# The lower parts of the weights after the attention: a subtraction on VectorE becomes a negation on ScalarE and an adding DMA

## The chip, the cores and the metric

The kernel runs on one core of one Trainium2 chip. The metric is the device time in microseconds of one execution; two runs of the kernel before took 971.85 and 971.94 us (median 971.89). The profile shows one execution of the same program: its engines are PE (TensorE, with PEld for its weight loads), DVE (VectorE), ACT (ScalarE), POOL (GpSimd) and the DMA queues that SP, ACT and POOL issue to (SPq, ACTq, and POOL's own).

## The reference, cut to what matters

One layer of a decoder trunk with three parallel token mixers, all float32, for 512 tokens of 1024 channels:

```
h   = adaLN(RMSNorm(x); c)
P   = h @ W_in                      # 13,872 columns, shared out among the mixers and three merge gates
yA  = gated short convolution       (from P)
yB  = sparse attention, 16 heads    (from P)
yC  = chunked spatial gating        (from P)
m   = sum_i sigmoid(h @ W_g[i]) * (y_i @ W_br[i])      # i = A, B, C
out = x + gate(c) * RMSNorm(m @ W_out)
```

What counts here are the large products. Each is made from operands that are split into two float32r parts: an upper part (the value rounded to float32r) and a lower part (the value less its upper part). A product is then three float32r matmuls: upper by upper, upper by lower, lower by upper.

## The kernel before, in words

The work is a stream of units. A unit is one product with 256 columns of weights: two PSUM banks of 24 matmuls of 128x128 by 512 each, 48 matmuls in all (`chan`, lines 99 to 107; the units with the tokens on the partitions use `tok`, lines 109 to 118, with matmuls of 256 columns). While a unit's matmuls run, the next unit's weights are fetched and split. They come in four pieces of 128x2x256 float32 (256 KB): SP issues a load into one of three `raw` buffers (`load_w`, line 84); then `split` (line 70) makes the upper part `wh` on ACT (line 71) and the lower part `wl` on DVE (line 72), out of `raw` and `wh`. `wh` and `wl` of a unit have two buffers, so that a piece can be split only when the unit before the running one has read its weights to the end. In a unit with `chan`, piece q is first used by the matmuls of blocks k = 2q and 2q+1, and `wl` by the third matmul of each block (line 106).

`split` also serves other operands: attention weights, keys, and the mixers' outputs (`yh`, `yl`). PE's order is that in which the code is written; the order on ACT, DVE, POOL and the queues is made by a scheduler with its own timing model.

The program goes: start (norm, adaLN, first products), the attention with projections of `h` filled in between its steps, and, from line 726 on, a second half: eight units for branch A (four gates `u_gate`, four merges `u_merge`), four units `u_v2`, eight units `u_z2` and `u_u2`, eight units for branch B, eight for branch C, then the output projection with the weights `woh` and `wo2` (lines 925 to 958). Between branch A's units the second half also loads `ws`, which POOL masks (`affine_select`, line 857), and `bi` and `gpb`. During branch B, `gate` (line 884) loads 16 more pieces of 256 KB into `rawg`; during branch C, `load_wo` (line 909) loads eight pieces of `w_out`.

Names of lines that the prediction uses: 71 and 72 (the two instructions of `split`), 84 (loads of pieces), 102, 104, 106 (the three matmuls of `chan`), 747 (drain of a gate's bank on ACT), 857 (mask of `ws` on POOL).

Of the kernel before, what the change touches and what calls it, by code (L numbers as in the profile page):

```python
# [10 lines left out]
AF = mybir.ActivationFunctionType  # L11
OP = mybir.AluOpType
# [25 lines left out]
def hybrid_block(ctx, tc, x, c, g_pre, g_post, w_ada, b_ada, w_in, conv_w, conv_b, pos_ck, w_ck1, w_ck2,  # L38
                 pos_cv, w_cv1, w_cv2, ln_g, ln_b, w_s, b_s, w_br, w_out, out):
    nc = tc.nc  # L40
    act = nc.scalar.activation
    stt = nc.vector.scalar_tensor_tensor
    ts = nc.vector.tensor_scalar
    tt = nc.vector.tensor_tensor
# [5 lines left out]
    w_ada = w_ada[0]  # L50
# [17 lines left out]
    WP, RB = 2, 3  # L68
# [1 line left out]
    def split(dst_h, dst_l, src):  # L70
        act(dst_h, src, AF.Copy)  # L71
        tt(dst_l, src, dst_h, op=OP.subtract)  # L72

# [4 lines left out]
    def load_w(src, col):  # L78
        """Starts the load of 256 columns; what comes back with the tiles are the steps that split them."""
        w = w_tiles()  # L80
        steps = []
        for q in range(0, KT, WP):
            raw = wpool.tile([128, WP, 256], F, name="raw", bufs=RB)
            nc.sync.dma_start(raw, src[q * 128:(q + WP) * 128, col:col + 256].rearrange("(k p) c -> p k c", p=128))
            steps.append((w[0][:, q:q + WP, :], w[1][:, q:q + WP, :], raw))
        return w, steps

    def rsqrt(y, v, neg_half):
        """y = v ** -0.5 by Newton's steps from a bitwise first guess; all [128, n]."""
        ts(y.bitcast(I32), v.bitcast(I32), -0.5, 1597463007.0, op0=OP.mult, op1=OP.add)  # L90
        ts(neg_half, v, -0.5, None, op0=OP.mult)
        t = const.tile(list(y.shape), F, name="rsq_t", bufs=2)
        for _ in range(3):
            tt(t, y, y, op=OP.mult)
            tt(t, t, neg_half, op=OP.mult)
            stt(y, t, 1.5, y, op0=OP.add, op1=OP.mult)

# [1 line left out]
    def chan(ps, w, sub, rh, rl, ks=range(KT), m=128):  # L99
# [19 lines left out]

    # ================= pools of the first half =================  # L120
    att = ExitStack()
# [5 lines left out]

    # ================= start: rmsnorm, adaLN, h transposed =================
    crow = sp.tile([KT, 128], F, name="crow")
# [41 lines left out]
    def load_ada(n, part):  # L171
        """Columns of w_ada for scale and shift of the channels of group n."""
        k, cnt = groups[n]
        per = 4 // cnt
        wa = sp.tile([128, per, 2, cnt * 128], F, name="wa", bufs=6)
        for e, off in enumerate((D, 0)):
            nc.sync.dma_start(wa[:, :, e, :], w_ada[part * per * 128:(part + 1) * per * 128,
                                                    off + k * 128:off + (k + cnt) * 128].rearrange(
                "(k p) c -> p k c", p=128))
        for q in range(per):  # L180
            was[n, part * per + q] = wa[:, q]
# [16 lines left out]
    def root(i):  # L198
        """The steps of ssq's way to its inverse root."""
        if i == 0:  # L200
            ts(ssq, ssq, 1.0 / D, EPS, op0=OP.mult, op1=OP.add)
        elif i == 1:
            ts(rst.bitcast(I32), ssq.bitcast(I32), -0.5, 1597463007.0, op0=OP.mult, op1=OP.add)
            ts(nh, ssq, -0.5, None, op0=OP.mult)
        elif i % 3 == 2:
            tt(ssq, rst, rst, op=OP.mult)
        elif i % 3 == 0:
            tt(ssq, ssq, nh, op=OP.mult)
        else:
            stt(rst, ssq, 1.5, rst, op0=OP.add, op1=OP.mult)  # L210
# [24 lines left out]
    def ada(n, q):  # L235
        """A step of the sum over c's channels for group n."""
        if n not in accs:
            accs[n] = sp.tile([128, 2, groups[n][1] * 128], F, name="acc", bufs=2)
            ts(accs[n], was[n, q], csil[:, q:q + 1], None, op0=OP.mult)
        else:  # L240
            stt(accs[n], was[n, q], csil[:, q:q + 1], accs[n], op0=OP.mult, op1=OP.add)
# [28 lines left out]
    def product(k, j, p):  # L270
        """One of the three passes of block k's share of two blocks of channels."""
        for e in range(2):
            mm(first[j][e], w_first[j][p == 1][:, k, e * 128:e * 128 + 128], (hh, hh, hl)[p][:, k, :],  # L273
               start=(todo[j] == 3 * KT), stop=(todo[j] == 1))
        todo[j] -= 1
# [21 lines left out]

    # ================= constants and long-lived tiles of the attention =================
    D0 = const.tile([128, S], F, name="D0")
# [56 lines left out]

# [1 line left out]
    class Stream:  # L358
# [20 lines left out]
        def step(self, last=False):  # L379
            """One matmul further; False at the end (or at that of the unit, if it is the last)."""  # L380
            while True:
# [26 lines left out]
        def to(self, n):  # L408
            """Through the first n units."""
            while self.n < n or (self.n == n and self.gen is not None):  # L410
                if not self.step(self.n == n):
                    break
# [10 lines left out]
    def w_vg():  # L423
        """The window's values and the gates' logits, side by side."""
        w = (gv.tile([128, KT, 304], R, name="wvh"), gv.tile([128, KT, 304], R, name="wvl"))
        steps = []
# [30 lines left out]

    # ================= compressed keys and values, among the projections =================
    def cmp_hidden(b):
# [45 lines left out]

    # ================= attention =================
    keep = ctx.enter_context(tc.tile_pool(name="keep", bufs=1, side="right", reuse_waits="tile"))
# [10 lines left out]

    # gated convolution branch (as twice its value)
    def u_cg(w, j):  # L520
# [22 lines left out]
    def u_silu(w, j, ys):  # L543
        """ys times twice the silu of the projection."""
        for e in range(2):
            b = 2 * j + e
            ps = acc_tile()
            yield from chan(ps, w, e, hh, hl)
            th = wk.tile([128, S], F, name="th", bufs=2)
            act(th, ps, AF.Tanh, scale=0.5)  # L550
            stt(th, th, 1.0, ps, op0=OP.add, op1=OP.mult)
            tt(ys[b], ys[b], th, op=OP.mult)
# [13 lines left out]

    # the keys of a group: for each branch 32 places for the compressed ones (the selected branch has them)
    # and then its own, upper parts and lower parts
    def k_stack(g, b):
# [34 lines left out]

    # the compressed branch's weights, transposed: a partition for each key, four times: upper and lower
    # parts of the even and of the odd blocks of queries; the rest of a row stays zero
    pcs = [wk.tile([128, NB // 2, 2, 128], R, name=f"pc{n}") for n in range(2)]
# [16 lines left out]
    def scores(u, i):  # L624
        """The scores of the queries' block i; for the first block those of both branches at once."""
        h, b = divmod(u, 2)
# [3 lines left out]
        ks = kst[h // HPG]  # L630
        # a bank has no room for the last block's compressed scores: they are with the first's
        o = 32 if b == 0 and i < NB - 1 else 0
# [54 lines left out]

    # the projections that run among the attention's steps, and the one that can only follow them
    base = len(stream.units)
# [8 lines left out]

    # positions of a unit's steps (head and branch), in periods from the unit's first
    POS = dict(S0=-1.301, S1=-0.333, S2=-0.131, S3=0.070, T0=0.701, T1=0.875, V0=1.510, V1=1.562, T2=1.261, T3=1.137, V2=1.802, V3=1.872, CS=0.718, CT=0.622, CO=1.177, HO=1.920, QS=-2.289, K0=-3.502, K1=-3.559)  # L700
# [22 lines left out]
    stream.to(len(stream.units))  # L723
    att.close()

    # ================= merge of the branches =================
    po = ctx.enter_context(tc.tile_pool(name="po", bufs=1, reuse_waits="tile"))
# [45 lines left out]

    # ================= gated spatial branch (as twice its value) =================
    def gelu_tanh(ps):
# [100 lines left out]

    # ================= the other branches; gate of the layer, times g_post =================
    fin = ctx.enter_context(tc.tile_pool(name="fin", bufs=1, reuse_waits="tile"))
# [44 lines left out]

    # ================= output projection, rmsnorm, residual =================
    wo2 = []
# [8 lines left out]
    for t in range(NB):  # L934
# [4 lines left out]
        bank = [acc_tile() for _ in parts]  # L939
        # as the parts come: their squares' sums, and their products with the gates  # L940
        for n, (cs, ps, wh, wl) in enumerate(zip(
# [47 lines left out]
```

## Time and profile before

| | |
|---|---|
| runs | 971.85 and 971.94 us |
| span of the profiled execution | 969.5 us; the runs' median is 2.4 us above it |
| PE busy | 939.7 us (97%) |
| DVE busy | 640.3 us (66%) |
| ACT busy | 447.7 us (46%) |
| POOL busy | 13.4 us (1%) |
| granted TensorE clock, mean | 0.999 |

The span is the time from the first to the last instruction of the profiled execution; the runs' time also holds what lies around it. Busy shares are means over the whole program, so the stages have to be read apart. The DMA engines' busy share is that of the core's 16 engines together. A wait is put down to the instruction that ended it.

### The profile page before, as it was taken

How to read it: one execution, taken by the hardware profiler on the slowest of the kernel's cores; microseconds unless marked ns; L12 is line 12 of the kernel's file. 1: busy time of each engine (PE TensorE's matmuls, PEld its weight loads, DVE VectorE, ACT ScalarE, POOL GpSimd, SP SyncE). 2: the span in 40 equal slices, each digit the busy share in tenths (PEclk: the TensorE clock that was granted, in tenths of full speed). 3: DMA queues.
4: the chain of work that ended last, by engine and by line, in shares of the span. 5: the costliest groups of instructions: out<-in, count | busy, mean ns of one | idle time of the engine just before them, and what ended most of it. 6: DMA issues, size and time to landing. Idle time of an engine off the chain costs nothing.

```text
span 969.5 us, 13657 instructions
## 1 busy us (share of the span) xinstructions
PE 939.7 (97%) x4833; PEld 797.1 (82%) x4833; DVE 640.3 (66%) x1641; ACT 447.7 (46%) x982; POOL 13.4 (1%) x38
## 2 busy tenths in 40 slices
PE   2999999999999999999999999999999999999996
PEld 1788978888887888888888888998888888888896
DVE  5863387998998889989855325666554654844443
ACT  5552366676666656666534224333333323523311
POOL 2010000000000000000000000000000000000000
PEclk9999999999999999999999999999999999999999
DMA  9963112222131221213134333233335545432312
GB/s 288 310 173 102 44 44 71 61 56 76 44 88 44 58 74 47 85 44 88 44 88 152 92 114 92 84 90 95 87 88 157 180 141 152 151 90 87 98 59 94
DMA packets 98569, 97.76 MB, mean 101 GB/s; under 512 B 6808, under 2 KB 93956, under 8 KB 98500
## 3 DMA queue, kind: packets, MB, share of 16 engines
q1 hardware_dynamic: 96132, 92.51, 32.8%
q10 hardware_dynamic: 2048, 4.19, 1.3%
q8 instruction: 38, 0.62, 0.3%
q14 instruction: 31, 0.25, 0.1%
q0 software_dynamic: 320, 0.17, 0.1%
HBM read 94.76 MB, written 2.10 MB: 100 GB/s over the span
## 4 chain that ended last, share of the span: by engine, by line
PE 92%; DMA 4%; DVE 2%; ACT 1%; SPq 1%; issue 0%; DVEq 0%; ACTq 0%
PE g L102 21%; PE g L104 21%; PE g L106 21%; PE o L678 4%; PE t L667 4%; PE s L645 3%; PE g L113 2%; PE g L117 2%; PE g L115 2%; DMA wa<-in_w_ada_dram 2%; PE s L463 2%; PE g L947 2%; PE g L948 2%; PE g L946 2%; PE f L273 2%; PE t L821 1%
## 5 line engine op out<-in xcount | busy, mean ns | idle before, releaser
L102 PE MATMUL g<-hh,wh 128*128 128x512 f32 x720 | 286.6, 398 | 0.0
L104 PE MATMUL g<-hl,wh 128*128 128x512 f32 x720 | 286.1, 397 | 0.0
L106 PE MATMUL g<-hh,wl 128*128 128x512 f32 x720 | 285.8, 397 | 0.0
L71 ACT ACTIVATE wh<-raw 128x512 fp32r<-128x512 f32 x252 | 146.0, 624 | 241.4 <-PE g L104 129.0
L72 DVE TENSOR_TENSOR wl<-raw,wh 128x512 fp32r<-128x512 f32 x252 | 165.3, 687 | 138.3 <-ACT wh L71 130.5
L106 PEld LDWEIGHTS g<-hh,wl 128*128 128x128 f32 x720 | 135.5, 188 | 24.3
L102 PEld LDWEIGHTS g<-hh,wh 128*128 128x128 f32 x720 | 135.4, 188 | 24.3
L104 PEld LDWEIGHTS g<-hl,wh 128*128 128x128 f32 x720 | 135.4, 188 | 24.1
L657 ACT ACTIVATE p<-p,mx 128x384 f32<-128x384 f32 (+3 forms) x128 | 71.1, 557 | 37.1 <-DVE mx L655 36.4
L102 PE MATMUL g<-yh,wh 128*128 128x512 f32 x192 | 75.4, 393 | 0.0
L104 PE MATMUL g<-yl,wh 128*128 128x512 f32 x192 | 74.7, 389 | 0.0
L106 PE MATMUL g<-yh,wl 128*128 128x512 f32 x192 | 74.7, 389 | 0.0
L655 DVE CUSTOM_DVE_ANT_0 p<-s,D 128x384 f32<-128x384 f32 (+3 forms) x128 | 60.7, 484 | 15.9 <-PE s L645 15.1
L71 ACT ACTIVATE ph<-t 128x512 fp32r<-128x512 f32 (+3 forms) x128 | 55.7, 435 | 32.7 <-PE t L667 31.4
L72 DVE TENSOR_TENSOR pl<-t,ph 128x512 fp32r<-128x512 f32 (+3 forms) x128 | 61.9, 485 | 4.6 <-ACT ph L71 3.4
L667 PE MATMUL t<-ident,p 128*128 128x128 f32 x320 | 57.0, 276 | 0.5 <-DVE pl L72 0.5
L660 DVE TENSOR_SCALAR p<-p,mx,gates 128x384 f32<-128x384 f32 (+3 forms) x128 | 55.5, 442 | 1.5
L645 PE MATMUL s<-kst,qst 128*128 128x288 f32 (+2 forms) x192 | 50.0, 342 | 1.2 <-DVE mx L655 1.2
L113 PE MATMUL g<-wh,hh 128*128 128x256 f32 x160 | 46.1, 288 | 0.0
L667 PEld LDWEIGHTS t<-ident,p 128*128 128x128 f32 x320 | 38.5, 140 | 8.7 <-DVE pl L72 0.6
L115 PE MATMUL g<-wl,hh 128*128 128x256 f32 x160 | 45.3, 283 | 0.0
L117 PE MATMUL g<-wh,hl 128*128 128x256 f32 x160 | 45.3, 283 | 0.0
(227 smaller groups left out, 1346.0 us busy)
## 6 DMA issues: line engine op xcount, KB each, us to landing
raw<-in_w_in_dram SPq DMA_DIRECT2D x204, 256.0 KB, 2.9
raw<-in_w_br_dram SPq DMA_DIRECT2D x48, 256.0 KB, 3.1
wa<-in_w_ada_dram SPq DMA_DIRECT2D x32, 256.0 KB, 6.2
rawg<-in_w_ada_dram SPq DMA_DIRECT2D x16, 256.0 KB, 3.4
rawf<-in_w_in_dram SPq DMA_DIRECT2D x6, 512.0 KB, 6.7
xt<-in_x_dram SPq DMA_DIRECT2D x4, 512.0 KB, 5.3
xr<-in_x_dram ACTq DMA_DIRECT2D x4, 512.0 KB, 6.3
rawg<-in_w_out_dram SPq DMA_DIRECT2D x8, 256.0 KB, 2.7
```

Of the source, the lines that this page charges most:

```text
L71: act(dst_h, src, AF.Copy)
L72: tt(dst_l, src, dst_h, op=OP.subtract)
L102: mm(ps, w[0][:, k, cs], rh[:, k, :], start=(k == 0), stop=False)
L104: mm(ps, w[0][:, k, cs], rl[:, k, :], start=False, stop=False)
L106: mm(ps, w[1][:, k, cs], rh[:, k, :], start=False, stop=(k == KT - 1))
L113: mm(ps, sh[:, k, cs], w[0][:, k, :n], start=(k == 0), stop=False)
L115: mm(ps, sh[:, k, cs], w[1][:, k, :n], start=False, stop=False)
L117: mm(ps, sl[:, k, cs], w[0][:, k, :n], start=False, stop=(k == KT - 1))
L645: mm(s_[:, :o + n], q[:, i * 128:(i + 1) * 128], ks[:, z, b, 32 - o:32 + n], start=(z == 0), stop=(z == 1))
L655: nc.vector.tensor_tensor_reduce(out=p, in0=s_, in1=D0[:, S - n:], scale=-slopes[h], scalar=LIM, op0=OP.add, op1=OP.min, accum_out=mx[:, 0 ...
L657: act(p, p, AF.Exp, bias=mx[:, 0, i:i + 1], scale=-1.0, accum_out=mx[:, 1, i:i + 1])
L667: nc.tensor.transpose(t_[:, (i - j) * 128:(i - j + 1) * 128], ps[i][:, j * 128:(j + 1) * 128], ident)
```

## The change

After the attention, a switch `by_dma[0]` is set. From then on `load_w` hands the piece's address in memory to `split`, and `split` makes the lower part in two steps: ACT writes the negative of the upper part into `wl`, and a DMA issued by POOL reads the piece from memory a second time and adds it to what stands in `wl`. The loads into `raw` stay. The switch covers the 36 units of the second half and the two units of `wo2`, 38 x 4 = 152 pieces; all other uses of `split` keep the subtraction on DVE. Comments were taken out as well, which moves line numbers by some lines.

```diff
-    def split(dst_h, dst_l, src):
+    by_dma = [False]
+
+    def split(dst_h, dst_l, src, at=None):
+
         act(dst_h, src, AF.Copy)
-        tt(dst_l, src, dst_h, op=OP.subtract)
+        if at is None:
+            tt(dst_l, src, dst_h, op=OP.subtract)
+        else:
+            act(dst_l, dst_h, AF.Copy, scale=-1.0)
+            nc.gpsimd.dma_start(dst_l, at, accum_op=OP.add)
...
             raw = wpool.tile([128, WP, 256], F, name="raw", bufs=RB)
-            nc.sync.dma_start(raw, src[q * 128:(q + WP) * 128, col:col + 256].rearrange("(k p) c -> p k c", p=128))
-            steps.append((w[0][:, q:q + WP, :], w[1][:, q:q + WP, :], raw))
+            at = src[q * 128:(q + WP) * 128, col:col + 256].rearrange("(k p) c -> p k c", p=128)
+            nc.sync.dma_start(raw, at)
+            steps.append((w[0][:, q:q + WP, :], w[1][:, q:q + WP, :], raw) + ((at,) if by_dma[0] else ()))
...
     att.close()
+    by_dma[0] = True
```

In the kernel with the change, `act(dst_h ...)` stands on line 74, the negation on line 78 and the adding DMA on line 79.

**ACT, at the weights of branch A's second gate.** `wh_5684` (with the change `wh_5692`) are that unit's upper parts, `th` is the drain of the first gate's second bank, and the last rows are the first pieces of the merge after it. Before:

```order
L71 ACTIVATE wh_5684<-raw_5686 128x512
L71 ACTIVATE wh_5684<-raw_5688 128x512
L71 ACTIVATE wh_5684<-raw_5690 128x512
L747 ACTIVATE th_5682<-g_5655 128x512
L71 ACTIVATE wh_5684<-raw_5692 128x512
L71 ACTIVATE wh_5754<-raw_5756 128x512
```

With the change:

```order
L74 ACTIVATE wh_5692<-raw_5694 128x512
L74 ACTIVATE wh_5692<-raw_5696 128x512
L74 ACTIVATE wh_5692<-raw_5698 128x512
L756 ACTIVATE th_5690<-g_5662 128x512
L78 ACTIVATE wl_5693<-wh_5692 128x512 x3
L74 ACTIVATE wh_5692<-raw_5700 128x512
L78 ACTIVATE wl_5693<-wh_5692 128x512
L74 ACTIVATE wh_5766<-raw_5768 128x512
```

The three first negations stand behind all three upper parts and behind the drain; the fourth stands behind the fourth upper part.

**POOL, from the end of the attention on.** `yx` belongs to the attention's half, `ws` is the spatial weights' mask, `wl_5601` the lower parts of branch A's first merge. Before:

```order
L577 MEMSET kst_3908 128x2x32
L523 MEMSET yx_4418 128x2
L523 MEMSET yx_4522 128x2
L857 AFFINE_SELECT ws_6113<-ws_6113 128x1024
L984 UNCONDITIONAL_BRANCH
```

With the change:

```order
L531 MEMSET yx_4522 128x2
L79 DMA wl_5579<-in_w_in_dram 128x2x256 x4
L79 DMA wl_5601<-in_w_br_dram 128x2x256 x3
L866 AFFINE_SELECT ws_6145<-ws_6145 128x1024
L79 DMA wl_5601<-in_w_br_dram 128x2x256
L79 DMA wl_5693<-in_w_in_dram 128x2x256 x4
```

POOL had one instruction left after the attention; now it has the 152 adding DMAs too, and the mask of `ws` stands ahead of the fourth piece of the first merge.

## Rows read from the trace of the kernel before

**Rows 1.** The page: busy us (share of the span) and instructions of each engine.

```profile
PE 939.7 (97%) x4833; PEld 797.1 (82%) x4833; DVE 640.3 (66%) x1641; ACT 447.7 (46%) x982; POOL 13.4 (1%) x38
```

**Rows 2.** Stages: length, busy us of PE, PEld, DVE, ACT, POOL, clock, DMA share, GB/s.

```profile
511.00:598.00 87.00, 87.00 (x386) 72.04 (x385) 35.59 (x56) 31.70 (x57) 2.25 (x1) 1.00 0.38 115
598.00:647.00 49.00, 49.00 (x400) 47.95 (x399) 27.88 (x51) 18.67 (x34) 0.00 (x0) 1.00 0.32 87
647.00:742.00 95.00, 95.00 (x453) 79.84 (x452) 57.15 (x99) 33.95 (x60) 0.00 (x0) 1.00 0.33 90
742.00:830.00 88.00, 88.00 (x389) 72.56 (x388) 51.10 (x96) 28.31 (x49) 0.00 (x0) 1.00 0.55 167
830.00:917.00 87.00, 87.00 (x386) 72.02 (x385) 41.78 (x66) 30.09 (x53) 0.00 (x0) 1.00 0.36 109
917.00:969.50 52.50, 45.00 (x289) 40.98 (x287) 23.49 (x83) 9.50 (x29) 0.00 (x0) 0.98 0.22 76
```

**Rows 3.** Waits from 497 us on: engine, line, releaser, total us, times, longest.

```profile
DVE wl L72 <- ACT wh L71: 120.0, 50, 5.9
ACT wh L71 <- PE g L104: 118.3, 28, 6.1
...
PEld g L102 <- DVE th L815: 0.4, 1, 0.4
```

**Rows 4.** Timeline of the tail: start, us, engine, line, operation.

```profile
961.73 0.28 PE L948 MATMUL g<-wh,mg 128*128 128x256 f32 x1
...
965.85 1.00 SPq L958 DMA_DIRECT2D out_dram<-ot  x2
```

**Rows 5.** Instructions on the pieces (`raw`) from 500 to 930 us, ns min/median/max.

```profile
L71 ACT ACTIVATE wh<-raw x152: 613/622/636, 500.1 to 921.3; 128x512 fp32r<-128x512 f32 x152
L72 DVE TENSOR_TENSOR wl<-raw,wh x152: 680/686/694, 501.0 to 921.9; 128x512 fp32r<-128x512 f32 x152
```

**Rows 6.** Timeline of ACT over one unit of branch A.

```profile
532.53 1.68 ACT L71 ACTIVATE wh<-raw 128x512 fp32r<-128x512 f32 x3 [5.95 <-PE g L104]
536.78 0.63 ACT L71 ACTIVATE wh<-raw 128x512 fp32r<-128x512 f32 x1 [2.57 <-DMA raw<-in_w_br_dram]
...
543.41 1.68 ACT L71 ACTIVATE wh<-raw 128x512 fp32r<-128x512 f32 x3 [4.62 <-PE g L104]
```

**Rows 7.** Timeline of POOL: what an issue of a DMA took.

```profile
4.42 0.52 POOL L145 DMA_DIRECT2D rows<-in_ln_b_dram  x1
...
52.73 1.12 POOL L327 DMA_DIRECT2D w<-in_w_ck_dram  x2 [46.05 <-PE tp L246]
```

**Rows 8.** DMA issues: count, KB each, median us from issue to landing.

```profile
raw<-in_w_br_dram SPq DMA_DIRECT2D x48, 256.0 KB, 3.1
...
w<-in_w_cv_dram POOLq DMA_DIRECT2D x2, 32.0 KB, 3.2
```

**Rows 9.** Stretches with known transfers, columns as in Rows 2.

```profile
0.00:20.00 20.00, 2.68 (x10) 1.96 (x10) 8.79 (x37) 9.42 (x17) 5.64 (x17) 1.00 0.98 283
523.00:534.00 11.00, 11.00 (x50) 9.09 (x50) 3.93 (x8) 3.22 (x6) 0.00 (x0) 1.00 0.33 97
...
965.00:969.50 4.50, 0.00 (x0) 0.00 (x0) 1.45 (x3) 0.00 (x0) 0.00 (x0) 0.72 0.31 117
```

**Rows 10.** Timeline around the mask of `ws` and the first merge's matmuls.

```profile
515.01 0.44 ACTq L856 DMA_DIRECT2D ws<-in_w_s_dram  x1
...
519.93 2.25 POOL L857 TENSOR_SCALAR_AFFINE_SELECT ws<-ws 128x1024 f32<-128x1024 f32 x1 [130.55 <-DMA ws<-in_w_s_dram]
...
521.68 0.39 PE L102 MATMUL g<-yh,wh 128*128 128x512 f32 x1
...
526.21 0.39 PE L106 MATMUL g<-yh,wl 128*128 128x512 f32 x1
```

## The prediction

> **What bounds the kernel now.** I read the page's busy line first: PE is busy 97% of the span, DVE 66%, ACT 46%, POOL 1% [rows 1]. That is a mean, so I cut the second half, the only part that the change touches, into its stages [rows 2]: branch A (511 to 598 us), the units `u_v2` (to 647), `u_z2` and `u_u2` (to 742), branch B (to 830), branch C (to 917), and the output. In the first five PE's busy time equals the length of the stretch, at a granted clock of 1.00: it never stands still. The waits say the same from the other side [rows 3]: DVE waits 120.0 us for ACT's upper parts, ACT waits 118.3 us for PE to give a weight buffer free, and PE's longest wait that a tile causes is 0.4 us. So the split of the weights already stands wholly behind the matmuls, and DVE's time there is not what the kernel waits for. What follows the last matmul (961.73 us) is the row's norm and the store [rows 4]; none of it is a split.
>
> **What the change takes away.** 152 subtractions of 0.686 us leave DVE [rows 5]: 152 x 0.686 = 104 us of DVE's 237 us after 511 us (the sum of its column in [rows 2]). Value for the end: nothing, since PE does not wait for DVE. The bounds of this gain are 0 and the odd half microsecond of [rows 3]; I take 0.
>
> **What it adds to ACT.** 152 negations over the same 128x512. Their nearest row is the upper part's, 0.622 us [rows 5]: 152 x 0.622 = 95 us, on top of the 152 us that ACT is busy in these 458.5 us [rows 2]. That is a third going to a half, hidden by ACT's waits for PE. What matters is the order. The unit in [rows 6] shows the period: a buffer comes free at 532.53, and the unit that reads it starts 10.9 us later, when the next buffer comes free (543.41). In the new order three upper parts (1.68 us), a drain (0.6 us at most) and then the first negation (0.6 us) end at 535.4. POOL issues the DMA, which must have landed by 543.4 and a half. Piece four: its upper part at 536.8 [rows 6], its negation done by 538.1, and its first use is the third matmul of block 6, which in [rows 10] comes 526.21 - 521.68 = 4.5 us behind its unit's start, so at 547.9. The DMAs thus have about 8 us for the first piece and 9.8 us for the fourth, issue included.
>
> **What it adds to POOL.** 152 issues. A DMA issue on POOL took 0.52 us for 8 rows and 0.56 us for 128 [rows 7]. A piece has 256 rows: by that slope 0.6 us. Four per unit are 2.4 of 10.9 us, hidden by POOL's idleness. No adding DMA is in the trace; from its issue to landing the nearest rows are 3.2 us for POOL's 32 KB and 3.1 us for SP's 256 KB [rows 8]. Even 5 us fits in 8. So one unit by itself does not stall.
>
> **One place where POOL's order matters.** The mask of `ws` (2.25 us, 519.93 to 522.18, waiting for a load issued at 515.01) now stands ahead of the first merge's fourth adding DMA. Issue at 522.2, 0.6 us, landing about 3.2 us after that begins or ends: 525.4 to 526.0, and if the load of `ws` is later by a microsecond among the new transfers, 527. The first matmul that needs it is due at 526.21 [rows 10]. Bounds 0 and 5 us (a landing of 8 us, two and a half times the 3.2); I take 1 us.
>
> **The DMA engines: the term that decides.** What does one adding DMA cost them? Price of a plain load: a steady unit has four loads in 11 us at a share of 0.33 [rows 9], so 0.33 x 11 / 4 = 0.91 us of all 16 engines; the start, at a share of 0.98 and 283 GB/s, gives 19.6 us for 5.66 MB, again 0.91 us per 256 KB. So this is what a load occupies, not an effect of low load. Price of reading SBUF: the two stores at the end are 0.31 x 4.5 = 1.40 us, 0.70 us each [rows 9]. An adding DMA must read the piece and what stands in `wl`, and write the sum. Lower bound: 0.91 us, if the second read costs nothing. Upper bound: 2.5 us, a load, a store and once more a load. I take a load plus a read of SBUF, 0.91 + 0.70 = 1.6 us.
>
> Each stage then has, as DMA busy time, its share by its length [rows 2] plus 1.6 us per piece (32 pieces; 16 in `u_v2`):
> - branch A: 33.1 + 51.2 = 84.3 of 87 us;
> - `u_v2`: 15.7 + 25.6 = 41.3 of 49;
> - `u_z2`, `u_u2`: 31.4 + 51.2 = 82.6 of 95;
> - branch B, with 16 loads of `rawg` besides: 48.4 + 51.2 = 99.6 of 88, **11.6 us too much**;
> - branch C: 31.3 + 51.2 = 82.5 of 87.
>
> In branch B the weights come late, and PE waits for the sum of what does not fit; the `rawg` loads cannot slip into branch C, because PE's own order has their products at the units' ends. The other stages fit, closely.
>
> Sum: 0 (DVE) + 0 (ACT) + 0 (POOL) + 1 (mask) + 12 (branch B) = +13 us against the profiled span of 969.5, so a span of 982.5; the runs' median of 971.89 stands 2.4 us above that span, which gives **985 us**.
>
> The Trainium skill, "Collectives: The Full Stack", section "The bandwidth ceiling: the fold count and why AG ≠ RS ≠ AR", says that an add in the DMA path is slow for its two source reads and not for the arithmetic, with 1.93 times a copy's time measured. By it a piece would cost 1.93 x 0.91 = 1.75 us, an estimate, and the sum would be about +20 us. No row here shows an adding DMA.
>
> **The rivals.**
> - *The DMA engines have room.* If an adding DMA costs 0.91 to 1.4 us, branch B has 48.4 + 32 x 0.91 = 77.5 of 88 us (93 at 1.4, 5 us over). Only the mask's microsecond and little else is left: 973 us, up to 978. For it: reads of the two sources could overlap, and the engines idle two thirds of the time in four stages. Against: at 0.91 us the second read and its write-back would be free. Chance 0.25.
> - *The DMA engines become the bound, slower by over 2%.* The place is branches A and B first; the point from which it decides is where the sum passes 19 us, which it does at 1.75 us per piece (branch A 2, branch B 16, and 1 for the mask). At 1.81 us, twice a load, it is +4 in branch A, +18 in branch B, +2 in branch C: 997 us. At 2.5 us it is 26 + 7 + 16 + 40 + 24 = +113 us: 1086 us. For it: three of five stages are already above 0.9 in my own sum, and an engine near full makes each landing later than the 3 us used above. Against: both sources are read in rows of 1 KB or more, and SBUF reads were the cheaper ones. Chance 0.35.
> - *POOL becomes the bound.* An issue of over 2.75 us (a fourth of 10.9) would leave PE waiting for POOL in each of 36 units: at 3.5 us, 4 x 3.5 - 10.9 = 3.1 us a unit, +112 us, 1084 us. Against it stand the 0.52 and 0.56 us of [rows 7], though none of those adds. Chance 0.04.
> - *Faster.* A lighter DVE would have to end a wait of PE's, and there is none over 0.4 us. Chance 0.01.
>
> **How the numbers follow.** The forecast, 1.4 to 1.75 us per piece, has the remaining 0.35 and gives 976 to 991. About 2% (19 us) is what a measurement of this kernel can tell from no change. Within it lie the forecast and the first rival, 0.35 + 0.25 = 0.60; slower by more are the two bounds on DMA and POOL, 0.39; faster 0.01. The range goes from 971 (everything hidden) to 1060 us, which is 2.3 us per piece by the same sum (+88 us); beyond lie the upper end of the price and a bound on POOL, together some 0.12. The likeliest case's own range is 976 to 991.
>
> **What would show it.** In the changed kernel: DVE's busy time down by about 104 us, ACT's up by about 95; the adding DMAs with a landing of 4 to 6 us in branches A and C and longer in branch B; a DMA share in branch B at 0.9 or above; waits of PE's line 106 (now 114) for `wl`, some 12 us in branch B and about 1 us at the first merge, and none in `u_v2`. PE waits spread evenly over all units would mean that a unit's landing, not the engines' load, decides; waits with a DMA share well under 0.9 would refute the price by shares; a POOL busy without a gap would be the third rival; no waits at all the first.

## The result and the profile after

The changed kernel takes **984.0 us** (median of two runs, 982.74 and 985.27) against 971.89 us: a ratio of **1.0124, 95% interval 1.0105 to 1.0143**. It is slower by a little over one per cent. The forecast was 985 us.

The profile is that of the execution of 985.27 us; its span is 983.6 us, 14.1 us longer than before. First the page's busy line, its DMA line over 40 slices of 24.6 us, and its rows of the queues: q1 carries SP's and ACT's loads, q0 the DMAs that POOL issues.

```profile
PE 944.3 (96%) x4833; PEld 796.5 (81%) x4833; DVE 548.7 (56%) x1489; ACT 527.3 (54%) x1134; POOL 197.2 (20%) x190
...
DMA  9963112121221213121269999899999999999942
...
q1 hardware_dynamic: 96132, 92.51, 32.1%
q0 software_dynamic: 41664, 40.03, 27.5%
```

Against [rows 1], DVE is busy 91.6 us less, ACT 79.6 us more, POOL 183.8 us more, and PE the same but for 4.6 us. (The first two are under the 104 and 95 us of count times duration, since neighbours on an engine overlap by some tens of ns: the row of the 152 negations has 87.5 us busy.) From slice 22 on the DMA engines are nearly always busy. The stages (columns as in [rows 2], their bounds moved by the delay): branch A, `u_v2`, `u_z2` with `u_u2`, branch B, branch C, output.

```profile
511.00:600.00 89.00, 87.47 (x386) 71.78 (x385) 15.33 (x25) 48.60 (x89) 40.05 (x33) 1.00 1.00 208
600.00:650.00 50.00, 50.00 (x403) 48.76 (x402) 18.92 (x35) 28.26 (x52) 19.47 (x16) 1.00 0.89 171
650.00:746.00 96.00, 96.00 (x457) 80.70 (x456) 38.23 (x67) 51.86 (x96) 41.04 (x35) 1.00 0.94 184
746.00:840.00 94.00, 87.08 (x371) 68.40 (x370) 30.11 (x60) 40.66 (x73) 36.70 (x31) 1.00 1.03 230
840.00:930.00 90.00, 89.98 (x397) 73.90 (x396) 24.44 (x39) 49.28 (x90) 38.93 (x32) 1.00 1.02 206
930.00:983.60 53.60, 44.80 (x286) 40.51 (x284) 20.67 (x79) 10.74 (x32) 4.87 (x4) 0.95 0.36 96
```

PE, which never stood still in the first five stages of [rows 2], now has 6.9 us of gaps in branch B and 1.5 us in branch A. Where they lie is read from PEld, the weight loads. These are the waits of line 114 (106 before) for a lower part, at the beginning of branch A and of branch B: start, us, the instruction, and in brackets how long it waited and for what.

```profile
524.67 0.19 PEld L114 LDWEIGHTS g<-yh,wl 128*128 128x128 f32 x1 [1.67 <-DMA wl<-in_w_br_dram]
527.99 0.19 PEld L114 LDWEIGHTS g<-yh,wl 128*128 128x128 f32 x1 [0.70 <-DMA wl<-in_w_br_dram]
...
754.83 0.19 PEld L114 LDWEIGHTS g<-yh,wl 128*128 128x128 f32 x1 [1.06 <-DMA wl<-in_w_br_dram]
757.03 0.19 PEld L114 LDWEIGHTS g<-yh,wl 128*128 128x128 f32 x1 [0.98 <-DMA wl<-in_w_br_dram]
759.27 0.19 PEld L114 LDWEIGHTS g<-yh,wl 128*128 128x128 f32 x1 [1.02 <-DMA wl<-in_w_br_dram]
761.45 0.19 PEld L114 LDWEIGHTS g<-yh,wl 128*128 128x128 f32 x1 [0.96 <-DMA wl<-in_w_br_dram]
769.49 0.19 PEld L114 LDWEIGHTS g<-hh,wl 128*128 128x128 f32 x1 [1.38 <-DMA wl<-in_w_in_dram]
772.27 0.19 PEld L114 LDWEIGHTS g<-hh,wl 128*128 128x128 f32 x1 [1.56 <-DMA wl<-in_w_in_dram]
774.44 0.19 PEld L114 LDWEIGHTS g<-hh,wl 128*128 128x128 f32 x1 [0.95 <-DMA wl<-in_w_in_dram]
776.58 0.19 PEld L114 LDWEIGHTS g<-hh,wl 128*128 128x128 f32 x1 [0.92 <-DMA wl<-in_w_in_dram]
```

They come in three clusters: two pieces of the first merge of branch A (weights `w_br`), all four pieces of the first merge of branch B, all four of its second gate (weights `w_in`). A wait of 1 us for a piece says that the four pieces arrive one after the other, each a little late. Later in branch B four more waits add up to 3 us.

A wait of PEld is not yet a delay of the end, since PE keeps a few matmuls in hand. The delay is read by taking the same matmul in both timelines (the last column takes the differences):

| what has been reached | before | after | delay | added there |
|---|---|---|---|---|
| last matmul of the attention | 499.25 | 499.02 | -0.2 | |
| first spatial transposes, `u_v2` | 609.51 | 611.43 | 1.9 | branch A 2.1 |
| matmul in `u_u2` | 715.58 | 717.49 | 1.9 | 0.0 |
| gate sum of `gate(3)`, end of branch B | 829.67 | 841.55 | 11.9 | branch B 10.0 |
| last matmul of the stream | 916.77 | 929.07 | 12.3 | branch C 0.4 |
| last matmul of the kernel | 961.73 | 975.51 | 13.8 | output 1.5 |

So 10.0 of the 14.1 us are lost in branch B. Behind the two clusters at its beginning, at the gate sum of `gate(0)` (773.75 us before, 783.07 after), the delay is 9.3 us; 7.4 of the 10.0 us are lost up to there and 2.6 in the rest of the branch. The adding DMAs themselves: minimum, median and maximum of POOL's issue (ns) and from the issue to the landing (us), then the median landing of each kind.

```profile
L79 POOL DMA_DIRECT2D wl<-in_w_in_dram x96: 1186/1687/2666, 503.0 to 902.8; - x96
...
DMA to landing us min/median/max: 4.2/7.0/14.9
```

```profile
wl<-in_w_in_dram POOLq DMA_DIRECT2D x96, 256.0 KB, 7.0
raw<-in_w_br_dram SPq DMA_DIRECT2D x48, 256.0 KB, 3.8
wl<-in_w_br_dram POOLq DMA_DIRECT2D x48, 256.0 KB, 7.5
```

An issue takes 1.69 us, a landing 7 us, and at worst 14.9. What one piece costs the DMA engines comes from q0: 27.5% of 983.6 us, over 152 pieces, is **1.78 us of all 16 engines**, 1.96 times the 0.91 us of a load [rows 9].

Why these two clusters? For the first merge of branch B: POOL issued its four DMAs from 743.83 on (the row below). From 744.08 on SP issued three `rawg` loads, at 744.51 and 745.17 ACT the loads of `gpo` and of the first `xr` (512 KB each), and at 745.67 SP the `raw` load of the second gate's third piece. The four adding DMAs then landed 11.0 to 14.9 us after their issue, and that `raw` load after 15.3 us (the first row below, from the chain that ended last). For the second gate, three timelines of the stretch that follows, SP, ACT and POOL (start, us; the bracket is the idle time before and its releaser):

```profile
745.67 15.31 DMA raw<-in_w_in_dram
```

```profile
755.21 5.10 SPq L898 DMA_DIRECT2D rawg<-in_w_ada_dram  x3
760.36 0.46 SPq L92 DMA_DIRECT2D raw<-in_w_in_dram  x1
```

```profile
753.54 1.15 ACT L74 ACTIVATE wh<-raw 128x512 fp32r<-128x512 f32 x2 [4.62 <-PE g L112]
...
761.00 0.63 ACT L74 ACTIVATE wh<-raw 128x512 fp32r<-128x512 f32 x1 [5.82 <-DMA raw<-in_w_in_dram]
761.54 1.66 ACT L78 ACTIVATE wl<-wh 128x512 fp32r<-128x512 f32 x3
```

```profile
743.83 4.87 POOL L79 DMA_DIRECT2D wl<-in_w_br_dram  x4 [6.01 <-ACT wl L78]
762.45 4.89 POOL L79 DMA_DIRECT2D wl<-in_w_in_dram  x4 [13.76 <-ACT wl L78]
```

Two upper parts were ready at 754.7. But ACT's order puts the third upper part ahead of all three negations, and its data landed only at 761.0, out of the same crowd of transfers as the first merge's pieces. So no piece of this gate was negated before 761.5, nearly 7 us after the first two could have been, and POOL, idle for 13.76 us, issued all four in one run. The `rawg` loads on SP that stand there from 755.21 on hold back the fourth piece only: its `raw` load was issued at 760.36, and its upper part waited another 1.05 us for it.

### The profile page after: what moved, and what is told of

The parts are those of the page before. It is cut to its first block, busy times and chain, and to the rows that moved or that the text cites. A ratio compares the mean times of both kernels' runs of the same rounds, so it can differ in the third digit from the quotient of the medians.

```text
span 983.6 us, 13868 instructions
## 1 busy us (share of the span) xinstructions
PE 944.3 (96%) x4833; PEld 796.5 (81%) x4833; DVE 548.7 (56%) x1489; ACT 527.3 (54%) x1134; POOL 197.2 (20%) x190
## 3 DMA queue, kind: packets, MB, share of 16 engines
q0 software_dynamic: 41664, 40.03, 27.5%
## 4 chain that ended last, share of the span: by engine, by line
PE 84%; DMA 10%; DVE 2%; ACT 2%; POOL 1%; issue 1%; SPq 1%; DVEq 0%; ACTq 0%
PE g L114 19%; PE g L110 19%; PE g L112 19%; PE o L686 4%; PE t L675 4%; PE s L653 3%; PE g L121 2%; PE g L125 2%; PE g L123 2%; DMA wa<-in_w_ada_dram 2%; PE s L471 2%; DMA wl<-in_w_br_dram 2%; DMA raw<-in_w_in_dram 2%; PE f L281 2%; PE g L956 1%; PE g L957 1%
## 5 line engine op out<-in xcount | busy, mean ns | idle before, releaser
L79 POOL DMA_DIRECT2D wl<-in_w_in_dram x96 | 116.7, 1775 | 270.1 <-ACT wl L78 156.0
L78 ACT ACTIVATE wl<-wh 128x512 fp32r<-128x512 f32 x152 | 87.5, 621 | 1.0
L76 DVE TENSOR_TENSOR wl<-raw,wh 128x512 fp32r<-128x512 f32 x100 | 65.6, 685 | 18.9 <-ACT wh L74 11.3
L79 POOL DMA_DIRECT2D wl<-in_w_br_dram x48 | 58.2, 1685 | 77.1 <-ACT wl L78 77.1
L663 DVE CUSTOM_DVE_ANT_0 p<-s,D 128x384 f32<-128x384 f32 (+3 forms) x128 | 60.7, 483 | 15.4 <-PE s L653 14.6
L114 PEld LDWEIGHTS g<-yh,wl 128*128 128x128 f32 x192 | 36.0, 188 | 15.8 <-DMA wl<-in_w_br_dram 8.4
```

The source lines that it names most:

```text
L78: act(dst_l, dst_h, AF.Copy, scale=-1.0)
L79: nc.gpsimd.dma_start(dst_l, at, accum_op=OP.add)
L114: mm(ps, w[1][:, k, cs], rh[:, k, :], start=False, stop=(k == KT - 1))
L663: nc.vector.tensor_tensor_reduce(out=p, in0=s_, in1=D0[:, S - n:], scale=-slopes[h], scalar=LIM, op0=OP.add, op1=OP.min, accum_out=mx[:, 0 ...
```

## The experiments

Two theories stood against each other. **Theory 1**, the prediction's: the DMA engines' busy time decides, so a stage whose loads and adding DMAs exceed its length is stretched by the excess. **Theory 2**: each piece has a deadline, and what decides is when its DMA is issued and how long that one takes to land; it comes late where ACT's or SP's order delays the issue, or where other loads are issued with it. Each experiment was timed beside the kernel before; the ratios are to that. In the diffs, minus is the changed kernel.

Where the runs below lost their time is read from the same four matmuls of each profiled execution, as a delay against the kernel before (499.25, 609.35, 916.77 and 961.73 us there): the attention's last matmul, with which the stretch under test begins; the first transpose of `ws`, after branch A; the stream's last matmul, after branches B and C; the kernel's last matmul. The first column is the delay that an execution brings along, the next three what is added to it.

| kernel | brought along | branch A | B and C | output | sum |
|---|---|---|---|---|---|
| changed | -0.2 | 2.1 | 10.4 | 1.5 | 13.8 |
| only the negation | 0.4 | 0.0 | -0.3 | 0.0 | 0.1 |
| plain copy | 2.0 | 2.2 | -0.3 | 0.0 | 3.9 |
| every other piece | 0.1 | 1.0 | 3.2 | 0.0 | 4.3 |
| branch B by VectorE | 1.0 | 3.0 | 0.8 | 1.3 | 6.1 |
| no `rawg` | 0.4 | 3.0 | 4.6 | 1.3 | 9.3 |
| no `gpo`, `xr` | 0.1 | 4.5 | 7.5 | 1.1 | 13.2 |
| neither | -0.2 | 2.4 | 0.6 | 1.6 | 4.4 |
| no `bi`, `gpb` | -0.1 | 4.0 | 11.7 | 1.9 | 17.6 |
| no mask | 0.3 | 3.9 | 6.9 | 1.1 | 12.2 |
| adding DMA at chosen places | -0.2 | 0.5 | 2.0 | 0.0 | 2.4 |

The table also shows how far one execution goes: branch A's code is the changed kernel's in four of these besides the first (branch B by VectorE, the three without `rawg`, `gpo` and `xr`), and its loss lies anywhere between 2.1 and 4.5 us. Branch B's code is unedited in the rows without `bi`, `gpb` and without the mask: 6.9 and 11.7 us beside 10.4. Differences smaller than that are not evidence.

**Only the negation.** The adding DMA is left out, so `wl` holds only the negative of the upper part.

```diff
             act(dst_l, dst_h, AF.Copy, scale=-1.0)
-            nc.gpsimd.dma_start(dst_l, at, accum_op=OP.add)
```

> The negations stay on ACT, the adding DMA is left out (so the lower parts are only the negative upper parts). Both theories: ACT's 95 us lie beside the matmuls, so 972 us (971 to 973). If the negations themselves, or their place in ACT's order, made PE wait, it would be above 975.

Measured: 971.25 us, ratio 0.9991 (0.9982 to 1.0001). No wait of PE for a lower part is left; branch B's DMA share is back at 0.52. DVE's relief and ACT's 95 us of negations together are worth nothing; the whole loss comes with the DMA.

**A plain copy in place of the add.** The DMA overwrites the negative with the weights, so the lower part is the weight itself.

```diff
-            nc.gpsimd.dma_start(dst_l, at, accum_op=OP.add)
+            nc.gpsimd.dma_start(dst_l, at)
```

> POOL's DMA copies the piece into the lower part's buffer in place of adding it (so the lower parts hold the whole weights): same bytes from memory, same 152 issues on POOL, no read of SBUF. Theory 1 (the DMA engines' busy time decides): 0.9 us per piece in place of 1.78, branch B 48 + 29 = 77 of 88 us, so 973 us. Theory 2 (a single piece's landing against its slack decides, through queues and bursts): the landing of 7 us falls to 4 or 5, the wait behind rawg's loads stays: 975 to 979 us, with waits of PE in branch B's second gate. The issue on POOL shows whether its 1.69 us are the 256 rows (stays) or the add (falls to 0.6).

Measured: 973.61 us, ratio 1.0013 (1.0004 to 1.0022). Rows of branch B's stage, of all waits for DMA from 497 us on, of the issue and of the landing:

```profile
742.00:832.00 90.00, 90.00 (x406) 74.84 (x405) 33.10 (x64) 45.60 (x82) 22.95 (x32) 1.00 0.91 255
```

```profile
PEld g L114 <- DMA wl<-in_w_br_dram: 2.5, 2, 2.2
```

```profile
L79 POOL DMA_DIRECT2D wl<-in_w_in_dram x96: 713/718/742, 505.2 to 893.4; - x96
...
DMA to landing us min/median/max: 3.2/5.0/10.6
```

The same 152 pieces on the same queue cost 1.7 us. In branch B they cost nothing; the two waits of the second row are branch A's, whose loss in this execution, 2.2 us, is that of the changed kernel. So it is branch B's loss that needs the add, and branch A's comes with a plain copy too. A copy lands in 5.0 us, its issue takes 0.72 us, and a piece costs 17.5% x 973.7 / 152 = 1.12 us of the engines. So the add itself has three prices: 0.66 us of the engines, 2 us of landing, 1 us of POOL. Branch B runs at a share of 0.91 and 255 GB/s without a gap. Of the numbers on record Theory 1's 973 us came; Theory 2's 975 to 979 us, with waits in the second gate, missed. Yet this run lowers all three prices at once: the first merge's four pieces landed 8.1 to 10.6 us after their issue, in place of 11.0 to 14.9, so that Theory 2 allows the time as well. It does not yet choose between the theories.

**Every other piece.** Only the first and third piece of a unit are made by the DMA, the others by VectorE.

```diff
-            steps.append((w[0][:, q:q + WP, :], w[1][:, q:q + WP, :], raw) + ((at,) if by_dma[0] else ()))
+            steps.append((w[0][:, q:q + WP, :], w[1][:, q:q + WP, :], raw) + ((at,) if by_dma[0] and q % 4 == 0 else ()))
```

> Only pieces 1 and 3 of a unit by negation and adding DMA, pieces 2 and 4 by DVE's subtraction. Theory 1: branch B 48.4 + 16 x 1.78 = 77 of 88 us, no stall, 972 to 973. Theory 2: bursts and order still catch single pieces, though landings are shorter: 974 to 978.

Measured: 976.3 us, ratio 1.0044 (1.0027 to 1.0060). Branch B's stage and PEld's waits in it:

```profile
742.00:832.00 90.00, 87.73 (x383) 71.20 (x382) 41.28 (x78) 35.02 (x63) 19.30 (x16) 1.00 0.83 204
```

```profile
PEld g L114 <- DMA wl<-in_w_in_dram: 2.7, 3, 1.7
PEld g L114 <- DMA wl<-in_w_br_dram: 1.5, 2, 1.2
```

Branch B still makes PEld wait 4.2 us, 3.3 of them at the same two places, and PE stands for 2.3 us, with the engines at 0.83 of the stage: at a lower share than the copy's 0.91, which made none. Theory 1 does not allow that.

**Branch B by VectorE.** From branch B's first merge to branch C's first gate the lower parts are VectorE's again.

```diff
     add_branch(2, yc, load_wo)
+    by_dma[0] = False
+    stream.to(n3 - 1)
+    by_dma[0] = True
     stream.to(n3)
```

> Branch B's units (from its first merge to branch C's first gate) split on DVE again, all else as changed. Both theories: the 10 us lost in branch B come back, 1.9 at the first merge and 1.5 at the output stay: 975 us (974 to 977). If the loss moved elsewhere, it would stay at 980 or more.

Measured: 977.3 us, ratio 1.0056 (1.0041 to 1.0070), just above the range expected: over half of the loss is gone with branch B. Left are branch A's loss, the output's, and under a microsecond behind them. Branch C has a share of 1.00 and no gap in PE from 832 to 919 us; branch A has 0.99 and loses 3.0 us. The load on the engines is nearly the same, and what is issued beside the pieces differs.

**ACT in the order of the code.** After the attention, ACT's instructions stay as written: each negation right behind its upper part.

```diff
     by_dma[0] = True
+    ctx.enter_context(tc.manual_schedule(engines={mybir.EngineType.PE, mybir.EngineType.Activation}))
```

> From the end of the attention ACT's order is the order of the code: each negation directly behind its upper part, and rawg's loads then stand between single loads of pieces on SP, not three together. The bytes are the same. Theory 1 (engines' busy time): branch B still loses about 10 us, 983 us. Theory 2 (queue order): the 5 us of branch B's second gate go, with the first negations out of the wait for the third piece, and the load of xr goes out of branch B's first burst: 974 to 978 us.

Measured: 1009.91 us, ratio 1.0376 (1.0358 to 1.0395). The expectation missed. The pairing came, but so did all the rest of the code's order. At branch B's start, in ACT's timeline:

```profile
745.01 0.63 ACT L789 ACTIVATE th<-th 128x512 f32<-128x512 f32 x1 [0.75 <-DVE th L788]
745.02 0.33 ACTq L889 DMA_DIRECT2D gpb<-in_b_ada_dram  x1
745.39 0.45 ACTq L891 DMA_DIRECT2D gpo<-in_g_post_dram  x1
745.88 0.63 ACT L74 ACTIVATE wh<-raw 128x512 fp32r<-128x512 f32 x1 [0.24 <-issue]
746.54 0.63 ACT L78 ACTIVATE wl<-wh 128x512 fp32r<-128x512 f32 x1
```

The upper parts of the gate whose matmuls were to start at 745 stood behind the last gelu of `u_u2`, and their adding DMAs were issued with `gpb`, `gpo` and three `rawg`. PEld then waited 8.3 us and PE stood for 7.9. The wait, and two stretches around its end (columns as in [rows 2]: the granted clock is the third number from the end):

```profile
755.17 0.28 PEld L114 LDWEIGHTS g<-hh,wl 128*128 128x128 f32 x1 [8.31 <-DMA wl<-in_w_in_dram]
```

```profile
747.00:754.00 7.00, 0.30 (x2) 0.00 (x0) 3.89 (x8) 2.47 (x5) 3.64 (x3) 0.65 1.00 292
754.00:757.00 3.00, 1.82 (x4) 1.49 (x5) 0.77 (x2) 1.09 (x2) 0.00 (x0) 0.50 1.19 232
```

This run says nothing on the pairing alone. What it shows fits Theory 2: with the same DMAs at a share of 1.02 from 746 to 840 us, a late issue at one place alone costs PE 7.9 us. The rest of the loss is spread: the last gate sum of branch B comes 26.7 us late, the last matmul 41.2 us, and there PE stands for another 7.9 us waiting for `wo2`'s lower parts.

**The loads beside them.** Five kernels take away what is issued next to the late pieces, or ahead of them on POOL. In the first the gate's 16 `rawg` loads are left out (it works on `gpo`'s data); in the second the loads of `gpo` and of the first `xr` (both constants then).

```diff
-                raw = fin.tile([128, 2, 256], F, name="rawg", bufs=3)
-                nc.sync.dma_start(raw, w_ada[q * 128:q * 128 + 256, 2 * D + 256 * j:2 * D + 256 * j + 256].rearrange(
-                    "(k p) c -> p k c", p=128))
+                raw = gpo[:, 0:512].rearrange("p (k c) -> p k c", k=2)
```

```diff
-    nc.scalar.dma_start(gpo, bass.AP(tensor=g_post.tensor, offset=g_post.offset, ap=[[0, 128], [1, D]]))
+    nc.vector.memset(gpo, 1.0)
...
-        nc.scalar.dma_start(xt, x[t * 128:(t + 1) * 128, :])
+        if t:
+            nc.scalar.dma_start(xt, x[t * 128:(t + 1) * 128, :])
+        else:
+            nc.vector.memset(xt, 0.0)
```

> The 16 loads of rawg are left out (the layer's gate is summed from other data). Theory 1: 16 x 0.91 = 14.6 us of DMA less, branch B fits, its 10 us go: 974 us. Theory 2: the wait of the second gate (5 us) goes with SP's queue free of them; the 4 us of the first merge stay in part, since gpo and xr are still loaded there: 975 to 978.

> The loads of gpo and of the first xr (512 KB each, issued together as branch B's first merge is being prepared) are left out, set to constants. Theory 1: 3.6 us of DMA less of 10 in branch B: 980 us. Theory 2: the four waits of the first merge (4.0 us) go, the four of the second gate (4.8 us) stay: 979 to 980 with that pattern of waits in the profile.

The third kernel has both edits:

> Leaves out both the gate's 16 rawg loads and the loads of gpo and of the first xr, each of which alone gave 979.0 and 986.1 us. If the losses of branch B simply add, 984 - 5 + 2 = 981 us. Theory 1: branch B's share falls to that of branch A (1.00) or a little under, which loses 2 us: 976 us. Theory 2: the first merge's adding DMAs land in 7 us instead of 11 to 15 and the second gate's third load is not behind others in SP's queue, so both groups of waits of branch B are gone together (under 1.5 us left of 10): 974 to 976 us, what is left being the first merge of branch A (2 us) and the output (1 us).

Measured: without `rawg` 978.96 us, ratio 1.0070 (1.0054 to 1.0086); without `gpo` and `xr` 986.07 us, 1.0147 (1.0126 to 1.0169); without any of them 978.04 us, 1.0055 (1.0036 to 1.0073). The profiled executions took 980.84, 984.9 and 976.09 us. All three medians lie above Theory 2's ranges, by 1 us, 6 us and 2 us, and above Theory 1's 974, 980 and 976 us; the places of the waits tell more than the times. In branch B (742 to 832 us) the first has the second gate's waits gone and the first merge's four left:

```profile
742.00:832.00 90.00, 87.54 (x391) 71.62 (x390) 29.75 (x59) 43.01 (x78) 38.38 (x32) 1.00 0.96 201
```

```profile
PEld g L114 <- DMA wl<-in_w_br_dram: 4.1, 4, 1.7
```

Its burst is no lighter at the first merge: where the gate's `rawg` loads stood, the scheduler has moved three loads of `w_out`, 256 KB each, up from branch C (SP issues them from 745.51 on), and the merge's four pieces landed 11.6 to 15.0 us after their issue. The second gate's pieces, issued only 1.3 us earlier than in the changed kernel, landed after 4.5 to 8.0 us in place of 7.0 to 10.7.

The second has its first merge's four waits gone, and its second gate has one long wait in place of four:

```profile
774.56 0.29 PEld L114 LDWEIGHTS g<-hh,wl 128*128 128x128 f32 x1 [3.14 <-DMA wl<-in_w_in_dram]
```

Here the third piece's `raw` load landed in time, and the wait is that of the fourth piece alone. Its `raw` load stood on SP behind four `rawg` loads (754.06 to 761.88), was issued at 761.93 and landed 5.5 us later; ACT waited 7.47 us for it, and POOL issued the adding DMA at 769.03.

The third has no wait of PEld in branch B, and PE without a gap:

```profile
742.00:832.00 90.00, 90.00 (x404) 74.75 (x403) 35.84 (x69) 46.37 (x85) 38.93 (x32) 1.00 0.97 197
```

The first and the third row are the pair that decides. Both have all 32 adding DMAs in branch B, and the engines at 0.96 and at 0.97. One makes PEld wait 4.1 us, the other not at all. What differs is 1 MB that is issued in the same microseconds as the first merge's pieces; the three `w_out` loads stand there in both. The landing of the first merge's four pieces goes with the waits: 11.0 to 14.9 us in the changed kernel and 11.6 to 15.0 without `rawg`, where PE waits; 7.1 to 10.9 without `gpo` and `xr`, 8.6 to 10.8 with neither group and 8.1 to 10.6 as a plain copy, where it does not. By the table branches B and C together lose 10.4 us with both groups of loads, 4.6 and 7.5 with one of them, 0.6 with neither; of these 7.5 alone lies within what unedited code shows. Theory 1 falls; Theory 2 stands for branch B. Bytes count in it too, but those in flight in a few microseconds and not a stage's sum. The second kernel's time missed my number: what it gained in branch B, its profiled execution lost in branch A, which the edit does not touch, and its runs lie at 984.9 to 989.6 us. The third's other runs reach 979.3 us; where those lose more is not known, as only one execution of a kernel is profiled.

**Branch A's first merge.** One kernel has constants in place of the loads of `bi` and `gpb`, the other leaves out the mask of `ws`, so that `ws` keeps its upper triangle.

```diff
-    nc.scalar.dma_start(bi.rearrange("p g i -> p (g i)"),
-                        bass.AP(tensor=b_s.tensor, offset=b_s.offset, ap=[[0, 128], [1, KT * 128]]))
+    nc.vector.memset(bi, 1.0)
...
-    nc.scalar.dma_start(gpb, bass.AP(tensor=b_ada.tensor, offset=b_ada.offset + 2 * D, ap=[[0, 128], [1, D]]))
+    nc.vector.memset(gpb, 1.0)
```

```diff
-    nc.gpsimd.affine_select(ws, ws, pattern=[[0, KT], [-1, 128]], compare_op=OP.is_ge, fill=0.0, base=0,
-                            channel_multiplier=1)
```

> The loads of bi and gpb (512 KB each, at the first merge of branch A) are left out, set to constants; the mask of ws on POOL stays. If the mask ahead of the fourth piece made the stall there, as predicted, piece four's wait (0.7 us) stays; if the burst of loads made it, both waits (1.67 and 0.70 us) go and the time is 982 us (2 us less).

> The mask of ws (2.25 us on POOL, ahead of the first merge's fourth adding DMA) is left out; its matrix then keeps its upper triangle. Theory 1 (the DMA engines' busy time decides): the mask moves no byte, so 984 us as before. Theory 2 (a piece's landing against its slack decides): the fourth piece's adding DMA is issued as soon as its negation is done, so the second of branch A's two waits (0.7 us in the changed kernel) goes and the first, for piece 2, stays at 1.7 us or grows by a part of it: 983 to 984 us, with one wait instead of two at the first merge of branch A. Branch B is untouched in both: 10 us lost.

Measured: 986.56 us, ratio 1.0151 (1.0108 to 1.0193), and 985.14 us, 1.0139 (1.0114 to 1.0165); neither gains. At the first merge each removes one of the two waits and the other one grows. Without the loads the fourth piece, behind the mask on POOL, waits 2.54 us (0.70 before the edit). Without the mask it is the second piece:

```profile
525.93 0.19 PEld L114 LDWEIGHTS g<-yh,wl 128*128 128x128 f32 x1 [2.38 <-DMA wl<-in_w_br_dram]
```

So which piece is late follows the edit each time, the second with the loads and the fourth with the mask. What each is worth is not settled: branch A's loss of 4.0 and 3.9 us lies within what unedited kernels show, and the two edits were not run together. Part of that loss is the clock: behind these longer waits the granted clock was 0.59 from 530 to 533 us and 0.56 from 527 to 530, while in the changed kernel it stayed at 1.00. The rest of the two times is branch B. Without the loads both clusters appear as before; without the mask the first merge keeps three of its waits, and the second gate has one of 0.62 us, since the third piece's `raw` load landed after 11.1 us and not 15.3.

**The DMA at chosen places.** The whole computation; VectorE subtracts in the first three units of branch A, from branch B's first merge to branch C's first gate, and in the output; the adding DMA makes the other 100 pieces.

```diff
     att.close()
-    by_dma[0] = True
...
+    n_a = len(stream.units)
     add_branch(0, ya)
...
+    stream.to(n_a + 2)
+    by_dma[0] = True
     stream.to(n0 - 1)
...
+    by_dma[0] = False
+    stream.to(n3 - 1)
+    by_dma[0] = True
     stream.to(n3)
...
     stream.to(len(stream.units))
+    by_dma[0] = False
```

> The computation is whole. The adding DMA stays where the changed kernel loses nothing with it (later units of branch A, u_v2, u_z2, u_u2, branch C: some 100 of 152 pieces); VectorE subtracts at the places where it waits (first units of branch A, branch B, the output's two column blocks). Theory 1: branch C at 32 pieces of 1.78 us and 31 us of its other transfers has 88 of 87 us, branch A less than its length: 973 to 975 us, DVE some 70 us less busy than in the kernel before. Theory 2: no piece is late where loads come in an even stream: 972 to 973.5 us, no wait for wl over 0.5 us outside the two places where the way of splitting switches. Neither theory gives a time under the kernel before, 971.9 us, since PE does not wait there.

Measured: 973.58 us, ratio 1.0016 (1.0006 to 1.0026). 100 of 152 pieces cost 1.6 us, clear of noise and a time just above Theory 2's 973.5; Theory 1's 973 to 975 us holds it too. Its profile has one wait of 1.6 us for VectorE's `th` and 1.7 us in four waits for DMAs. DVE is 60.7 us less busy than before, and it buys nothing.

## Why the prediction was right, and where it was not

- **PE bounds the second half, so DVE's relief is worth nothing: shown.** Without the DMA the time is 971.25 us.
- **ACT's 95 us are hidden: shown** by the same run; the negation took 0.62 us as its nearest row said. That a unit by itself leaves about 8 us holds in `u_v2`, `u_z2` and `u_u2`, where nothing was lost, and in branch C, where it was 0.4 us.
- **POOL's issue, 0.6 us: mis-sized.** It took 1.69 us; a copy of the same shape took 0.72. Four issues, 6.8 of a unit's 10.9 us, still hide. The slope from small DMAs was right for a copy, and nothing in the trace could show the add.
- **Landing of 3.1 to 5 us: mis-sized.** 7.0 us at the median, against 5.0 for the copy. Little is then left of the 8 us that a unit leaves its first piece, and at the crowded places it was 11 us and more.
- **The mask's microsecond: right place, half the story.** Branch A lost 2.1 us here and up to 4.5 in other runs, and 2.2 with a plain copy. The fourth piece, behind the mask on POOL, waited 0.70 us; the larger part, 1.67 us for the second piece, went only when the loads of `bi` and `gpb` did, which I had not counted.
- **12 us in branch B: right place and nearly right size (10.0), by a step that is wrong. That 985 us met 984.0 is luck.** My sum compared each stage's DMA busy time with its length. Put the measured 1.78 us in it (57 us for 32 pieces) and branches A, B and C overflow by 3, 17 and 1 us, 22 in all with the mask: 994 us. The price that I had taken, 1.6 us, was too low, and the rule that turns it into time was too harsh; the two errors nearly cancelled. A stage does not stall because its share is high (0.97 with no wait, 1.02 in branch C with 0.4 us lost), nor run free because it is lower (0.83 with 4.2 us). Branch B lost because its `rawg`, `gpo` and `xr` loads are issued in the same microseconds as the first merge's pieces and a `raw` load of the second gate, and because the upper part made from that load stands ahead of three negations on ACT. My text had the sentence that fits better, as a sign against the forecast: that a unit's landing would decide. I had expected such waits to be spread evenly; they are in clusters.
- **The Trainium skill's rule** ("Collectives: The Full Stack", section "The bandwidth ceiling: the fold count and why AG ≠ RS ≠ AR"): its 1.93 times a copy's time lies near the 1.96 loads measured here, where the load is SP's. Against a plain copy on the same queue as the add, 1.12 us, the trace has 1.59 times. The +20 us that I worked out from it did not come: the price of 1.75 us was close to the measured 1.78, and the step from price to time was wrong.
- **The output: not foreseen.** I costed the eight pieces of the last two column blocks at nothing; two waits there cost 1.5 us.
- **The rivals.** With a price at or above 1.75 us I had the kernel slower by over 2%. The price was passed and the loss stayed at 1.2%, so that rival failed for the same reason as the forecast's step.
- **Slips in my sums.** The likeliest case's lower end, 1.4 us per piece, gives 978 us by the same sum and not 976, and 2.3 us per piece gives +86 us and not +88. Neither bears on the outcome.

Open: what causes branch B's later waits (2.6 us of its loss), and what pairing each negation with its upper part would give, if the rest of ACT's order stayed.

## What to carry to other kernels

An extra DMA in a prefetched stream is judged by one piece's deadline: when its issue can start, behind what on its engine and on the queue of the loads that it depends on, and what else is issued in the same microseconds. A mean busy share over a stage tells neither that it stalls nor that it doesn't. And work taken off an engine that the bounding engine never waits for buys nothing, however much it is: 104 us of DVE were worth nothing here.

## What was not expected of the hardware

- The DMA busy share of a stretch can read above 1 (1.13 and 1.19 in some stretches of a few microseconds), so it is not read here as a fraction of a capacity.
- An add costs more than a second read: beside a copy's 1.12 us of the engines it takes 1.78, its issue on POOL 1.69 us at the median (from 1.19) instead of 0.72, and its landing 7.0 us instead of 5.0.
- A stall of PE has a price behind it. After PE had waited 8.3 us, its granted clock stood at 0.50, the lower level of 1.2 GHz, from 754 to 757 us, and at 0.60 in the next 3 us; after the wait of 3.14 us in the kernel without `gpo` and `xr` it was 0.70 on average from 775 to 780 us. Shorter stalls can have it too: after waits of 2.38 us (no mask) and 2.54 us (no `bi`, `gpb`), with PE idle for 2.0 and 2.1 us, it was 0.56 and 0.59 over 3 us, in part at the lower level. After 2.23 us in the plain copy and after waits of 0.9 to 1.6 us in branch B of the changed kernel it stayed at 1.00.
- One `raw` load took 15.3 us to land where the median is 3.2 to 3.8: it was issued behind three other loads on SP and within 3 us of two loads of 512 KB and four adding DMAs.
